# A hybrid trunk's state-space prologue: plain f32 input product, rotation tables on VectorE alone, 1/rms at the eviction, states turned back through the operators

## Chip, cores and metric

The kernel runs on one core of a Trainium2 chip. The metric is the device time of one execution in microseconds; the time before is the median of three runs. Engines are called as in the profile: PE is TensorE's matmul, PEld its weight load, DVE is VectorE, ACT is ScalarE, POOL is GpSimd, SP is SyncE, which issues most transfers.

## The reference

A decoder trunk of two layers over 1024 tokens of 1024 features, all in float32. Layer 0 mixes tokens with a diagonal state-space model (S5), layer 1 with sparse attention; a squared-ReLU MLP of width 4096 stands behind each, and each of the four parts is normalised before and after. What the change touches is the mixer of layer 0:

```python
def s5_mixer(h, w_in, ...):              # h = rms_norm(x, g)
    u = (h @ w_in).reshape(bsz, seq, 32 groups, 16 channels)
    abar = exp((lr + i li) dt)           # per group and state (64 states)
    bbar = (abar - 1) / (lr + i li) * b
    bu = einsum(u, bbar)
    xs = associative_scan(x_t = abar x_(t-1) + bu_t)
    y = einsum(xs.re, c.re) - einsum(xs.im, c.im) + d_skip * u
    z = gelu(y)
    z = z * sigmoid(z @ w_glu)
    return z @ w_out
```

The norm is `x * rsqrt(mean(x^2) + eps) * g`.

## The kernel before, in words

The program is written with a tile framework that orders each engine's instructions ahead of time and puts in the semaphores; on the chip each engine works its list in order and waits where a semaphore says so. A transfer is issued by an engine's queue, in order too.

The sequence is taken in 128 chunks of 8 steps. The S5 part (`s5`, L669 and on) does this:

- **Input product** (`s5_in`): for four pairs of steps `sp`, x times w_in, eight tiles of 128 features deep, 512 columns wide. Products of the kernel are made from two float32r parts per operand, (hi, lo), with three instructions each (`mm3`, L138 to L143: hi hi, hi lo, lo hi). ACT makes hi of x (L134) and of w_in with the norm's gain (L574); DVE or POOL make lo (L135, L575). The norm's 1/rms comes from squares of a token-major copy (L592, ACT) and a short chain on DVE and ACT (`rsqrt`, L149 to L153). For `sp` 0 to 2 it is put in later, in six DVE steps (L596); for `sp` 3 at the eviction from PSUM (L604).
- **Parameters** (`s5_params`): exponentials, cosines and powers of [128, 32] tiles, several hundred small DVE instructions (L331 to L491).
- **Rotations** (`s5_rotations`): tables of cosines and sines over the chunks, in seven doubling steps of three instructions (L509 to L511), each step on 16 m numbers per partition for m = 1, 2, 4, .., 64. Half 0 (for operators 0 and 2) is made on DVE, half 1 (for 1 and 3) on POOL. ACT spreads them (L513 to L515).
- **Operators** (`s5_operators`, four times, `o0` to `o3`): L525 to L527 on DVE, then 8 products of 16 columns (L535) and 8 transposes (L536) on PE; T by small transfers (L547) into a tile that POOL fills with zeros (L545); G on DVE (L550 to L552).
- **States** (`s5_states`, `s0` to `s3`): U transposed (L619), products with the operator (L627 to L629), turned into a rotating frame (L630 to L632), scanned along the chunks (L636), and turned back: two ACT copies swap the halves (L639, L640), POOL multiplies by the sines (L641), DVE by the cosines (L642) and subtracts (L643).
- **Outputs** (`s5_gelu`, `g0` to `g3`): per group a product with T (L654) and one with G (L655) into one bank, gelu (L657), transposes (L663).

Products with an f32 operand that is not split (L535, L627 to L629, L654, L655) are plain f32. The gate (`g` tiles) and the output product (`p` tiles on L141 to L143 from 190 us) end the mixer; norms follow, and from 260 us on MLP and attention.

Of the kernel before, what the change touches and what calls it, by code (L numbers as in the profile page):

```python
# [35 lines left out]
def bc_mid(t, shape):  # L36
    """[p, a, c] read as [p, a, n, c]."""
    return t.rearrange("p (a o) c -> p a o c", o=1).to_broadcast(shape)


def bc_last(t, shape):
    """[p, a, b] read as [p, a, b, n]."""
    return t.rearrange("p a (b o) -> p a b o", o=1).to_broadcast(shape)


class Trunk:
# [34 lines left out]
    def p1(self, shape):  # L81
        """One bank of PSUM."""
        self.n += 1
        return self.pp.tile(shape, F32, name=f"p1_{self.n}", tag="p1", bufs=7)

    def pm(self):
        """One bank of PSUM for the MLPs."""
# [3 lines left out]
    def pg(self):  # L91
        """One bank of PSUM for the gate's sums."""
# [3 lines left out]
    def small(self, shape, dt=F32, tag="s", bufs=8):  # L96
        """A few numbers of each partition, from a ring; more than a few in a tile of their own."""
# [13 lines left out]
    def unit(self, src, last=False):  # L111
        """A weight unit of 128 x 1024 as two halves of 512 columns, each split into two f32r parts."""
# [25 lines left out]
    def mm3(self, ps, w, x, start, stop):  # L138
        """ps += w.T x for operands (hi, lo)."""
# [5 lines left out]
    def rsqrt(self, ms, n, k=1.0):  # L145
        """k / sqrt of a [128, n] tile of normal positive numbers."""
# [9 lines left out]
    def pc(self):  # L156
        """One bank of PSUM for the norms."""
# [3 lines left out]
    def squares(self, blocks, add):  # L161
        """Sums of squares of the 512 tokens of four blocks [128, 2, 512], as [128, 4] in PSUM."""
# [18 lines left out]
    def pre_norm(self, h, gi, tag="b", square=True):  # L181
        """Blocks of h -> (hi, lo) blocks of h times the norm's gain, and 1/rms of the tokens, or its square, which
        goes in behind the products."""
# [19 lines left out]
    def post_norm(self, f, gi, h, e=None, reorder=False, last=None, aside=False):  # L203
        """h + norm(f) in place of the blocks f; reorder puts tokens (s, kk) into the order of time. Where f is still
        to be scaled by r, the square of a 1/rms, e is EPS / r^2 for the sum of squares: as norm(r f) is
        f / sqrt(mean(f^2) + EPS / r^2), r itself isn't needed."""
# [51 lines left out]
    def mlp(self, L, x, side=None, per=0, wait=0, finish=None):  # L258
        """side: a generator of other work, per of its steps beside each weight unit after the first ones. finish is
        called with each half of the tokens, whose last products come one half after the other."""  # L260
# [64 lines left out]
    def exp_(self, x, n):  # L325
        """exp of a [128, n] tile."""
# [73 lines left out]
    def s5_params(self, par, dsk, em, bc):  # L400
# [36 lines left out]
        # rows 0..63 hold real parts, 64..127 imaginary ones; sg flips signs between them  # L437
# [14 lines left out]
        # powers l = 0..8  # L452
# [19 lines left out]
        # unit phasor of a whole chunk, its powers 1, 2, 4, .., 64 (cos, and -sin and sin), and the chunk's decay;  # L472
        # rows 0..63 hold the phasors of groups 0..15, rows 64..127 those of the others
# [21 lines left out]
    def s5_rotations(self, A, B, k, eng):  # L495
        """Cosines and sines over the chunks for 8 groups in A and 8 in B: worked out in A with the groups of B in
        rows 64..127, then spread."""
# [19 lines left out]
    def s5_operators(self, o):  # L517
        """Operators of eight groups."""
# [9 lines left out]
        # H[(s, c), c'] of lag 7 - s, with d_skip at lag 0  # L528
# [24 lines left out]
        r["G"] = gm  # L553
        return r

    def s5_in(self, U):
        """norm(x) @ w_in by chunk, with the norm's gain in w_in and its 1/rms put in behind the product."""
        nc, a = self.nc, self.a
        xs, wu = [], []

        def load(sp):
            xs.append([self.ld([128, 4, 256], a["xs"][sp, dh]) for dh in range(2)])

        xs.append([self.ld([128, 4, 256], a["xs"][0, 0])])
        for j in range(4):
            if j == 1:
                xs[0].append(self.ld([128, 4, 256], a["xs"][0, 1]))
            self.n += 1
            raw = self.wp.tile([128, 1024], F32, name=f"wr{self.n}", tag="wr5", bufs=4)
            nc.sync.dma_start(raw, a["w_in"][j])  # L570
            kh, kl = [self.blk([128, 2, 512], F32R, tag="x") for _ in range(2)]
            for h in range(2):
                r, gn = raw[:, h * 512:(h + 1) * 512], self.gain[:, 0, 2 * j + h:2 * j + h + 1]
                nc.scalar.activation(kh[:, h], r, AF.Copy, scale=gn)  # L574
                nc.vector.scalar_tensor_tensor(kl[:, h], r, gn, kh.bitcast(F32)[:, h], op0=ALU.mult, op1=ALU.subtract)  # L575
                wu.append((kh[:, h], kl[:, h]))
        ms = self.small([128, 8], F32, "kept")
        us = U.rearrange("p g (s c) -> p s g c", c=16)

        def scaled(k, n):  # L580
            m = self.small([128, 8], F32)
            nc.vector.tensor_scalar(m[:, :n], ms[:, k:k + n], 1.0 / 1024, EPS, op0=ALU.mult, op1=ALU.add)
            return self.rsqrt(m, n)

        for sp in range(4):
            if sp:
                load(sp)
            x = [self.split(xs[sp][dh], [128, 4, 256], lo_pool=sp > 0 or dh > 0, tag="hid") for dh in range(2)]
# [4 lines left out]
            if sp == 3:  # L593
                ri = scaled(6, 2)
                for k in range(6):
                    nc.vector.tensor_scalar(us[:, k], us[:, k], r0[:, k:k + 1], None, op0=ALU.mult)  # L596
            for s_ in range(2):
                ps = self.pm()
                for kt in range(8):
                    self.mm3(ps, [t[:, kt % 4, s_ * 128:(s_ + 1) * 128] for t in x[kt // 4]], wu[kt], kt == 0, kt == 7)  # L600
                if sp < 3:
                    nc.scalar.activation(us[:, 2 * sp + s_], ps.rearrange("p (g c) -> p g c", c=16), AF.Copy)
                else:
                    nc.scalar.activation(us[:, 2 * sp + s_], ps.rearrange("p (g c) -> p g c", c=16), AF.Copy,  # L604
                                         scale=ri[:, s_:s_ + 1])
            if sp == 2:
                r0 = scaled(0, 6)
# [685 lines left out]
```

## Time and profile before

| | |
|---|---|
| runs | 2326.21, 2325.18, 2315.68 us; median 2325.18 |
| profiled execution, span from first to last instruction | 2320.5 us |
| profiled execution, a time of its own | none on the page; the span is 4.7 us under the median of the runs |
| PE, DVE, ACT, POOL busy | 94%, 64%, 48%, 40% |
| mean granted clock of TensorE | 0.973 |

The clock is given as a share of full speed; it has two levels, 2.4 GHz (1.0) and 1.2 GHz (0.5). Busy times overlap: PE's products are pipelined, and a product's row has its latency, so the distance between starts tells what one costs in a row of them.

### The profile page before, as it was taken

To read this page: it belongs to the slowest core of one execution; us is meant where nothing else is said; L and a number is where in the kernel's file an instruction comes from. 1 tells how busy PE (TensorE), PEld (TensorE's weight loads), DVE (VectorE), ACT (ScalarE), POOL (GpSimd) and SP (SyncE) were. 2 spreads that over 40 slices of the span, in tenths; PEclk is the share of its full clock that TensorE was granted. 3 is DMA by queue.
4 is the path that set the end of the run, shared out by engine and by line. 5 is a ranking of instruction groups with operands and counts; after the bars stand their busy time and mean duration, and the time that the engine had idled before them with its cause. 6 is when DMAs were issued, how large, how long until landed. Compare 5 with 4: busy or idle time off the path is not lost.

```text
span 2320.5 us, 31662 instructions
## 1 busy us (share of the span) xinstructions
PE 2186.8 (94%) x11392; PEld 1855.6 (80%) x11392; DVE 1481.9 (64%) x2949; ACT 1105.0 (48%) x2009; POOL 928.5 (40%) x752
## 2 busy tenths in 40 slices
PE   7688999999999999999999989899999998999997
PEld 5467778888879987888878977787889887788886
DVE  9875873233562499556595899999767738433335
ACT  5435543333354565455454666666455644333332
POOL 5422552222245533444347433444555435322223
PEclk9779999999999999999999999999999999999998
DMA  7102443333345554443455524233333245433331
GB/s 259 40 20 68 141 163 93 98 100 93 97 141 167 134 128 115 112 111 94 142 180 145 145 90 109 76 88 79 87 87 79 80 130 181 136 100 93 98 100 55
DMA packets 92988, 258.47 MB, mean 111 GB/s; under 512 B 10912, under 2 KB 23584, under 8 KB 92832
## 3 DMA queue, kind: packets, MB, share of 16 engines
q1 hardware_dynamic: 79072, 232.34, 31.4%
q0 software_dynamic: 12672, 23.07, 5.5%
q8 instruction: 90, 1.47, 0.3%
q10 hardware_dynamic: 1088, 1.05, 0.1%
q14 instruction: 66, 0.54, 0.1%
HBM read 222.73 MB, written 32.51 MB: 110 GB/s over the span
## 4 chain that ended last, share of the span: by engine, by line
PE 68%; DVE 18%; ACT 5%; issue 5%; POOL 1%; DMA 1%; SPq 0%; DVEq 0%; ACTq 0%; POOLq 0%
PE m L141 17%; PE m L142 17%; PE m L143 17%; PE p L141 2%; PE p L143 2%; PE p L142 2%; PE p L1021 2%; PE p L1042 2%; DVE wh L124 2%; DVE b L234 1%; ACT junk L962 1%; PE p L891 1%; DVE b L191 1%; DVE junk L924 1%; DVE acc L234 1%
## 5 line engine op out<-in xcount | busy, mean ns | idle before, releaser
L142 PE MATMUL m<-b,wh 128*128 128x512 f32 (+1 forms) x2208 | 859.1, 390 | 10.4 <-DVE b L191 7.8
L141 PE MATMUL m<-b,wh 128*128 128x512 f32 (+1 forms) x2208 | 860.6, 391 | 7.9 <-ACT acc L316 2.9
L143 PE MATMUL m<-b,wh 128*128 128x512 f32 (+1 forms) x2208 | 857.7, 390 | 3.4 <-DVE wh L124 3.4
L124 POOL TENSOR_TENSOR wh<-wr,wh 128x512 fp32r<-128x512 f32 x318 | 439.0, 1382 | 954.7 <-ACT wh L123 916.0
L123 ACT ACTIVATE wh<-wr 128x512 fp32r<-128x512 f32 x636 | 396.8, 628 | 493.6 <-PE m L143 407.0
L142 PEld LDWEIGHTS m<-b,wh 128*128 128x128 f32 x2208 | 418.0, 189 | 93.6 <-DVE b L191 10.8
L141 PEld LDWEIGHTS m<-b,wh 128*128 128x128 f32 x2208 | 417.7, 189 | 92.5 <-ACT acc L316 4.5
L143 PEld LDWEIGHTS m<-b,wh 128*128 128x128 f32 x2208 | 417.8, 189 | 85.9 <-DVE wh L124 3.8
L124 DVE TENSOR_TENSOR wh<-wr,wh 128x512 fp32r<-128x512 f32 x318 | 268.2, 844 | 311.7 <-ACT wh L123 280.4
L318 DVE TENSOR_TENSOR acc<-acc,m 128x512 f32<-128x512 f32 x216 | 147.1, 682 | 145.5 <-PE m L143 144.0
L1029 POOL TENSOR_TENSOR s<-s,ring 128x128 f32<-128x128 f32 (+7 forms) x128 | 157.7, 1244 | 161.5 <-DVE ring L1028 140.3
L283 ACT ACTIVATE b<-m 128x512 f32<-128x512 f32 x128 | 76.2, 595 | 152.9 <-PE m L143 152.3
L132 DVE CAST b<-b 128x1024 fp32r<-128x1024 f32 x68 | 64.5, 949 | 120.4 <-ACT b L285 117.3
L141 PE MATMUL p<-wh,b 128*128 128x256 f32 x480 | 135.8, 288 | 3.0 <-ACT wh L123 3.0
L142 PE MATMUL p<-wh,b 128*128 128x256 f32 x480 | 136.4, 288 | 1.6 <-POOL wh L124 1.2
L143 PE MATMUL p<-wh,b 128*128 128x256 f32 x480 | 135.4, 286 | 0.0
L1046 ACT ACTIVATE pt<-p 128x512 fp32r<-128x512 f32 (+1 forms) x160 | 83.3, 553 | 91.0 <-PE p L1042 84.9
L1027 ACT ACTIVATE s<-s,ring 128x128 f32<-128x128 f32 (+7 forms) x128 | 98.6, 772 | 50.8 <-DVE ring L1025 46.9
L1023 DVE CUSTOM_DVE_ANT_0 s<-p,nb 128x512 f32<-128x512 f32 (+3 forms) x192 | 100.3, 550 | 34.6 <-PE p L1021 29.8
L1047 DVE TENSOR_TENSOR pt<-p,pt 128x512 fp32r<-128x512 f32 (+1 forms) x160 | 99.0, 630 | 30.5 <-ACT pt L1046 30.1
L962 ACT ACTIVATE junk<-b,ring 128x512 bf16<-128x512 f32 (+2 forms) x90 | 80.8, 898 | 73.0 <-DVE ring L958 67.2
L1021 PE MATMUL p<-kt,q 128*128 128x256 f32 x640 | 104.9, 293 | 5.0 <-DVE acc L318 2.4
(306 smaller groups left out, 3229.2 us busy)
## 6 DMA issues: line engine op xcount, KB each, us to landing
wr<-in_w_dram SPq DMA_DIRECT2D x256, 512.0 KB, 3.6
wr<-in_wa_dram SPq DMA_DIRECT2D x32, 512.0 KB, 3.7
q<-qd POOLq DMA_DIRECT2D x64, 256.0 KB, 5.4
ld<-hd SPq DMA_DIRECT2D x24, 512.0 KB, 6.7
hd<-b SPq DMA_DIRECT2D x16, 512.0 KB, 4.5
qd<-qt SPq DMA_DIRECT2D x32, 256.0 KB, 3.4
wr<-in_wao_dram SPq DMA_DIRECT2D x16, 512.0 KB, 3.6
q<-qi POOLq DMA_DIRECT2D x24, 256.0 KB, 4.7
```

What stands on the lines that cost most here:

```text
L123: nc.scalar.activation(hi, r, AF.Copy)
L124: (nc.gpsimd if h else nc.vector).tensor_sub(lo, r, hi.bitcast(F32))
L141: mm(ps, w[0], x[0], start=start, stop=False)
L142: mm(ps, w[0], x[1], start=False, stop=False)
L143: return mm(ps, w[1], x[0], start=False, stop=stop)
L318: nc.vector.tensor_add(acc[d][:, j], acc[d][:, j], ps)
L962: nc.scalar.activation(junk[:, 1, :W[j]], keys[j].bitcast(F32), AF.Sign, bias=neg[:, j:j + 1], accum_out=cnt[:, j:j + 1])
L1021: nc.tensor.matmul(ps[:, 256 * e:256 * e + 256], qt[:, v, 2 * hp + k, :], self.K[2 * c + e][:, g, :], start=v == 0, stop=v == 1)
L1023: nc.vector.tensor_tensor_reduce(out=s[:, a:a + n], in0=ps[:, :n], in1=nb[:, a:a + n], scale=1.0, scalar=-BIG, op0=ALU.add, op1=ALU.max, a ...
L1027: nc.scalar.activation(s, s, AF.Exp, bias=ng[:, k, 0:1], scale=0.125, accum_out=sm[:, k, 0:1])
L1029: nc.gpsimd.tensor_tensor(s, s, rc[:, k, 0:1].to_broadcast([128, W]), op=ALU.mult)
L1047: nc.vector.tensor_sub(pl[:, :nk], pt[:, :nk], ph.bitcast(F32)[:, :nk])
```

## The change

Six things change, all in the S5 part; comments and docstrings are gone as well, so that lines from L596 of the old file on stand eight lower in the new one.

- The input product takes x and w_in (with the gain) as plain f32: one instruction where there were three, without splits of x and w_in. w_in gets the gain in place (ACT). x is loaded into the buffers that the splits had.
- 1/rms is worked out for each pair of steps and put in at each eviction from PSUM; the six DVE steps are gone.
- Both halves of the rotation tables are made on DVE.
- The sums of the turned states (old L632) are DVE's for all four sets.
- States are no longer turned back after the scan. DVE multiplies the scanned states by sines into one tile and by cosines in place; the swap of halves and the difference are left to PE, which adds a third product per group, with an operator `Gs` that is G with its halves swapped (two ACT copies per set of operators).
- `s5_states` returns that second tile too.

```diff
@@ s5_operators @@
-        r["G"] = gm
+        nc.scalar.activation(t[0:64], gm[64:128], AF.Copy)
+        nc.scalar.activation(t[64:128], gm[0:64], AF.Copy)
+        r["G"], r["Gs"] = gm, t
@@ s5_in @@
...
-            raw = self.wp.tile([128, 1024], F32, name=f"wr{self.n}", tag="wr5", bufs=4)
-            nc.sync.dma_start(raw, a["w_in"][j])
-            kh, kl = [self.blk([128, 2, 512], F32R, tag="x") for _ in range(2)]
+            w = self.blk([128, 2, 512], tag="x")
+            nc.sync.dma_start(w, a["w_in"][j].rearrange("p (h n) -> p h n", h=2))
             for h in range(2):
-                r, gn = raw[:, h * 512:(h + 1) * 512], self.gain[:, 0, 2 * j + h:2 * j + h + 1]
-                nc.scalar.activation(kh[:, h], r, AF.Copy, scale=gn)
-                nc.vector.scalar_tensor_tensor(kl[:, h], r, gn, kh.bitcast(F32)[:, h], op0=ALU.mult, op1=ALU.subtract)
-                wu.append((kh[:, h], kl[:, h]))
+                gn = self.gain[:, 0, 2 * j + h:2 * j + h + 1]
+                nc.scalar.activation(w[:, h], w[:, h], AF.Copy, scale=gn)
+                wu.append(w[:, h])
...
         for sp in range(4):
+            squares(sp)
             if sp:
                 load(sp)
-            x = [self.split(xs[sp][dh], [128, 4, 256], lo_pool=sp > 0 or dh > 0, tag="hid") for dh in range(2)]
...
-            if sp == 3:
-                ri = scaled(6, 2)
-                for k in range(6):
-                    nc.vector.tensor_scalar(us[:, k], us[:, k], r0[:, k:k + 1], None, op0=ALU.mult)
+            m = self.small([128, 8], F32)
+            nc.vector.tensor_scalar(m[:, :2], ms[:, 2 * sp:2 * sp + 2], 1.0 / 1024, EPS, op0=ALU.mult, op1=ALU.add)
+            r = self.rsqrt(m, 2)
             for s_ in range(2):
                 ps = self.pm()
                 for kt in range(8):
-                    self.mm3(ps, [t[:, kt % 4, s_ * 128:(s_ + 1) * 128] for t in x[kt // 4]], wu[kt], kt == 0, kt == 7)
...
+                    nc.tensor.matmul(ps, xs[sp][kt // 4][:, kt % 4, s_ * 128:(s_ + 1) * 128], wu[kt],
+                                     start=kt == 0, stop=kt == 7)
+                nc.scalar.activation(us[:, 2 * sp + s_], ps.rearrange("p (g c) -> p g c", c=16), AF.Copy,
+                                     scale=r[:, s_:s_ + 1])
@@ s5_states @@
-            (nc.gpsimd if o else nc.vector).tensor_add(z[:, s], z[:, s], t[:, s])
+            nc.vector.tensor_add(z[:, s], z[:, s], t[:, s])
...
-        Z, Zs, C, S = X[:, :, 1:128], t[:, :, 1:128], C[:, :, 0:127], S[:, :, 0:127]
-        nc.scalar.activation(Zs[0:64], Z[64:128], AF.Copy)
-        nc.scalar.activation(Zs[64:128], Z[0:64], AF.Copy)
-        nc.gpsimd.tensor_mul(Zs, Zs, S)
-        nc.vector.tensor_mul(Z, Z, C)
-        nc.vector.tensor_sub(Z, Z, Zs)
-        return ut, X
+        nc.vector.memset(t[:, :, 0:1], 0.0)
+        nc.vector.tensor_mul(t[:, :, 1:128], X[:, :, 1:128], S[:, :, 0:127])
+        nc.vector.tensor_mul(X[:, :, 1:128], X[:, :, 1:128], C[:, :, 0:127])
+        return ut, X, t
@@ s5_gelu @@
                 nc.tensor.matmul(py[:, i, :], X[:, g, :], r["G"][:, g].rearrange("p t c -> p (t c)"),
+                                 start=False, stop=False)
+                nc.tensor.matmul(py[:, i, :], Xs[:, g, :], r["Gs"][:, g].rearrange("p t c -> p (t c)"),
                                  start=False, stop=True)
@@ s5 @@
-        self.s5_rotations(*CS, 1, nc.gpsimd)
+        self.s5_rotations(*CS, 1, nc.vector)
```

The framework orders each engine's list anew, and in the mixer the lists differ beyond the lines edited. Behind the mixer they are the same but for a few neighbours on PE in one place.

On PE, the end of the input product (`m` tiles), the second operator (L535 and L536 into `p_85`, `p_87`) and the first transposes of U (L619), before:

```order
L143 MATMUL m_668<-b_115,b_621 128x512
L535 MATMUL p_85_699<-b_426,b_694 128x16
L536 MATMUL p_87_701<-con,b_694 128x128
L536 MATMUL p_88_711<-con,b_694 128x128
L619 MATMUL p_93_739<-con,U_84 128x128 x4
L627 MATMUL p_97_753<-b_738,b_512 128x128
```

The same place now; the second operator is `p_69`, `p_71`, `p_72`, and the input product L595 (each row x2 is two of a bank's eight instructions):

```order
L595 MATMUL m_196<-b_101,ld_188 128x512 x2
L535 MATMUL p_46_387<-b_302,b_382 128x16
L535 MATMUL p_69_531<-b_302,b_526 128x16
L536 MATMUL p_72_543<-con,b_526 128x128
L595 MATMUL m_206<-b_87,ld_186 128x512 x2
L595 MATMUL m_506<-b_87,ld_496 128x512 x2
L595 MATMUL m_516<-b_87,ld_496 128x512 x2
L595 MATMUL m_516<-b_101,ld_498 128x512 x2
L611 MATMUL p_77_573<-con,U_84 128x128 x4
```

The second operator stood behind the whole product; now three banks, 24 of its 64 instructions, stand behind the second operator.

On DVE, the last doubling step of the rotations and what follows it up to the second operator's L527, now (`b_428` is the table; before, one L509, L510 and L511 of each size stood here and the others on POOL):

```order
L509 TENSOR_TENSOR b_428<-b_428,tb_216 128x2x8x64
L510 TENSOR_TENSOR b_430<-b_428,tb_216 128x1024
L510 TENSOR_TENSOR b_460<-b_428,tb_216 128x1024
L511 TENSOR_TENSOR b_428<-b_428,b_430 128x2x8x64
L511 TENSOR_TENSOR b_428<-b_428,b_460 128x2x8x64
L550 TENSOR_TENSOR b_421<-tb_216,b_302 128x1024
L525 TENSOR_TENSOR b_526<-tb_216,b_301 128x1024
L527 TENSOR_TENSOR b_526<-b_526,b_527 128x1024
```

Both halves alternate on DVE in each step.

On DVE, between the scans of the first states (`b_787` before, `b_621` now) and those of the second, before and then now:

```order
L636 SCALAR_TENSOR_TENSOR b_787<-tb_340,b_751 128x127 x4
L630 TENSOR_TENSOR b_815<-p_107_817,b_550 128x512
L642 TENSOR_TENSOR b_787<-b_787,b_550 128x8x127
L636 SCALAR_TENSOR_TENSOR b_851<-tb_340,b_815 128x127 x4
L643 TENSOR_TENSOR b_787<-b_787,b_752 128x8x127
```

```order
L628 SCALAR_TENSOR_TENSOR b_621<-tb_216,b_585 128x127 x4
L622 TENSOR_TENSOR b_647<-p_91_649,b_428 128x512
L632 TENSOR_TENSOR b_586<-b_621,b_428 128x8x127
L624 TENSOR_TENSOR b_647<-b_647,b_648 128x512
L633 TENSOR_TENSOR b_621<-b_621,b_428 128x8x127
L628 SCALAR_TENSOR_TENSOR b_683<-tb_216,b_647 128x127 x4
```

What PE's outputs wait for was L643, between the second set's scans; it is now L633, ahead of all of them.

## Rows read from the trace of the kernel before

**Rows 1.** The page: busy us, mean ns of one, idle before.

```profile
L283 ACT ACTIVATE b<-m 128x512 f32<-128x512 f32 x128 | 76.2, 595 | 152.9 <-PE m L143 152.3
```

**Rows 2.** Busy time by stretch: engines, PEclk, DMA share, GB/s.

```profile
4.60:82.30 77.70, 55.88 (x216) 43.43 (x216) 76.58 (x204) 42.48 (x63) 52.00 (x32) 0.88 0.57 209
...
145.70:166.00 20.30, 19.78 (x85) 13.90 (x84) 15.33 (x17) 2.81 (x5) 6.78 (x4) 0.50 0.15 42
...
260.00:2320.50 2060.50, 1982.33 (x10410) 1694.77 (x10408) 1283.86 (x2579) 985.52 (x1828) 819.42 (x680) 0.99 0.38 112
```

**Rows 3.** Groups of DVE from 4.6 to 82.3 us, columns as rows 1.

```profile
L482 DVE TENSOR_TENSOR sb<-tb 128x16 f32<-128x16 f32 x9 | 7.7, 855 | 0.0
L511 DVE TENSOR_TENSOR b<-b,b 128x16 f32<-128x16 f32 (+6 forms) x7 | 7.4, 1054 | 0.0
L575 DVE SCALAR_TENSOR_TENSOR b<-wr,con,b 128x512 fp32r<-128x512 f32 x8 | 6.0, 748 | 0.8 <-ACT b L574 0.8
...
L509 DVE TENSOR_TENSOR b<-b,tb 128x16 f32<-128x16 f32 (+6 forms) x7 | 3.9, 557 | 0.0
...
L483 DVE TENSOR_TENSOR sb<-tb 128x16 f32<-128x16 f32 x9 | 1.5, 162 | 0.0
```

**Rows 4.** Groups of POOL in the same stretch.

```profile
L135 POOL TENSOR_TENSOR b<-ld,b 128x1024 fp32r<-128x1024 f32 x7 | 19.3, 2753 | 21.4 <-ACT b L134 21.4
L511 POOL TENSOR_TENSOR b<-b,b 128x16 f32<-128x16 f32 (+6 forms) x7 | 10.5, 1500 | 0.3
...
L545 POOL MEMSET b<- 128x1024 f32 x1 | 1.0, 956 | 0.0
```

**Rows 5.** PE in order of time, 82 to 123 us: start, duration, [idle before].

```profile
82.40 0.58 PE L535 MATMUL p<-b,b 128*128 128x16 f32 x2 [8.96 <-DVE b L527]
...
86.55 0.45 PE L536 MATMUL p<-con,b 128*128 128x128 f32 x1
...
91.23 1.97 PE L619 MATMUL p<-con,U 128*128 128x128 f32 x8 [4.23 <-ACT U L604]
...
101.31 0.49 PE L627 MATMUL p<-b,b 128*128 128x128 f32 x2 [0.25 <-ACT b L620]
...
107.61 0.71 PE L654 MATMUL p<-b,b 128*128 128x128 f32 x4
114.32 0.79 PE L655 MATMUL p<-b,b 128*128 128x128 f32 x2 [6.00 <-DVE b L643]
...
122.42 1.93 PE L535 MATMUL p<-b,b 128*128 128x16 f32 x16 [0.98 <-ACT b L664]
```

**Rows 6.** DVE in order of time, 96 to 114 us.

```profile
96.56 0.69 DVE L630 TENSOR_TENSOR b<-p,b 128x512 f32<-128x512 f32 x1 [6.83 <-PE p L627]
...
102.57 1.36 DVE L636 TENSOR_TENSOR_SCAN b<-tb,b 128x127 f32<-128x127 f32 x4
...
113.08 1.19 DVE L643 TENSOR_TENSOR b<-b,b 128x1016 f32<-128x1016 f32 x1
```

**Rows 7.** PE in order of time, 137 to 190 us.

```profile
137.55 0.39 PE L654 MATMUL p<-b,b 128*128 128x128 f32 x2
137.78 0.39 PE L655 MATMUL p<-b,b 128*128 128x128 f32 x2
...
144.67 0.37 PE L535 MATMUL p<-b,b 128*128 128x16 f32 x2 [2.49 <-DVE b L527]
...
152.43 0.74 PE L627 MATMUL p<-b,b 128*128 128x128 f32 x2
...
163.20 0.80 PE L142 MATMUL g<-b,wh 128*128 128x512 f32 x1
...
176.60 0.80 PE L655 MATMUL p<-b,b 128*128 128x128 f32 x2 [1.02 <-DVE b L643]
...
190.00 1.66 PE L141 MATMUL p<-b,wh 128*128 128x512 f32 x6 [0.82 <-ACT b L713]
```

**Rows 8.** POOL in order of time, 170 to 171 us.

```profile
170.47 3.32 POOL L641 TENSOR_TENSOR b<-b,b 128x1016 f32<-128x1016 f32 x1 [5.06 <-issue]
```

More of the change, by code (lines that the diff above doesn't have):

```diff
@@ L558, in s5_in, with squares @@
         nc, a = self.nc, self.a
-        xs, wu = [], []
+        xs, wu, sq = [], [], []
         def load(sp):
[L562 to L568, printed above, removed]
-            raw = self.wp.tile([128, 1024], F32, name=f"wr{self.n}", tag="wr5", bufs=4)
-            nc.sync.dma_start(raw, a["w_in"][j])
-            kh, kl = [self.blk([128, 2, 512], F32R, tag="x") for _ in range(2)]
-            for h in range(2):
-                r, gn = raw[:, h * 512:(h + 1) * 512], self.gain[:, 0, 2 * j + h:2 * j + h + 1]
-                nc.scalar.activation(kh[:, h], r, AF.Copy, scale=gn)
-                nc.vector.scalar_tensor_tensor(kl[:, h], r, gn, kh.bitcast(F32)[:, h], op0=ALU.mult, op1=ALU.subtract)
-                wu.append((kh[:, h], kl[:, h]))
[L577 to L587, printed above, removed]
-            x = [self.split(xs[sp][dh], [128, 4, 256], lo_pool=sp > 0 or dh > 0, tag="hid") for dh in range(2)]
+            xs.append([self.ld([128, 4, 256], a["xs"][sp, dh], "hid") for dh in range(2)])
+        def squares(sp):
             for s_ in range(2 * sp, 2 * sp + 2):
@@ L592, in s5_in @@
                 nc.scalar.activation(q, q, AF.Square, accum_out=ms[:, s_:s_ + 1])
-            if sp == 3:
-                ri = scaled(6, 2)
-                for k in range(6):
-                    nc.vector.tensor_scalar(us[:, k], us[:, k], r0[:, k:k + 1], None, op0=ALU.mult)
+        xs.append([self.ld([128, 4, 256], a["xs"][0, 0], "hid")])
+        for j in range(4):
+            if j == 1:
+                xs[0].append(self.ld([128, 4, 256], a["xs"][0, 1], "hid"))
+            w = self.blk([128, 2, 512], tag="x")
+            nc.sync.dma_start(w, a["w_in"][j].rearrange("p (h n) -> p h n", h=2))
+            for h in range(2):
+                gn = self.gain[:, 0, 2 * j + h:2 * j + h + 1]
+                nc.scalar.activation(w[:, h], w[:, h], AF.Copy, scale=gn)
+                wu.append(w[:, h])
+        ms = self.small([128, 8], F32, "kept")
+        us = U.rearrange("p g (s c) -> p s g c", c=16)
+        for sp in range(4):
+            squares(sp)
+            if sp:
+                load(sp)
+            m = self.small([128, 8], F32)
+            nc.vector.tensor_scalar(m[:, :2], ms[:, 2 * sp:2 * sp + 2], 1.0 / 1024, EPS, op0=ALU.mult, op1=ALU.add)
+            r = self.rsqrt(m, 2)
             for s_ in range(2):
@@ L599, in s5_in @@
                 for kt in range(8):
-                    self.mm3(ps, [t[:, kt % 4, s_ * 128:(s_ + 1) * 128] for t in x[kt // 4]], wu[kt], kt == 0, kt == 7)
[L601 to L607, printed above, removed]
+                    nc.tensor.matmul(ps, xs[sp][kt // 4][:, kt % 4, s_ * 128:(s_ + 1) * 128], wu[kt],
+                                     start=kt == 0, stop=kt == 7)
+                nc.scalar.activation(us[:, 2 * sp + s_], ps.rearrange("p (g c) -> p g c", c=16), AF.Copy,
+                                     scale=r[:, s_:s_ + 1])
             yield
@@ L637, in s5_states, with s5_gelu @@
                                          z[:, g, 0:127], 0.0, op0=ALU.mult, op1=ALU.add)
-        Z, Zs, C, S = X[:, :, 1:128], t[:, :, 1:128], C[:, :, 0:127], S[:, :, 0:127]
-        nc.scalar.activation(Zs[0:64], Z[64:128], AF.Copy)
-        nc.scalar.activation(Zs[64:128], Z[0:64], AF.Copy)
-        nc.gpsimd.tensor_mul(Zs, Zs, S)
-        nc.vector.tensor_mul(Z, Z, C)
-        nc.vector.tensor_sub(Z, Z, Zs)
-        return ut, X
-    def s5_gelu(self, o, r, ut, X):
+        nc.vector.memset(t[:, :, 0:1], 0.0)
+        nc.vector.tensor_mul(t[:, :, 1:128], X[:, :, 1:128], S[:, :, 0:127])
+        nc.vector.tensor_mul(X[:, :, 1:128], X[:, :, 1:128], C[:, :, 0:127])
+        return ut, X, t
+    def s5_gelu(self, o, r, ut, X, Xs):
         nc = self.nc
```

## The prediction

> **What bounds the kernel now.** I read the busy time by stage first [rows 2]. From 260 us to the end TensorE (PE) is busy 1982 of 2060 us: a product behind a product. None of that is edited, and on VectorE (DVE), ScalarE (ACT), GpSimd (POOL) and SyncE the order behind the mixer is the same in both kernels (on PE but for a few neighbours in one place), so what the prologue gives or takes moves the end one for one. The question is when the mixer's output products start: 190.0 us now [rows 7].
>
> Then DVE in the first stretch: from 4.6 to 82.3 us it is busy 76.6 of 77.7 us [rows 2]; its groups [rows 3] show why. L482 and L483 are the same 128x16 shape, yet one averages 855 ns and the other 162; the L511 steps of the rotations take 7.4 us for what L509 does in 3.9. Beside them POOL splits x and builds the second rotation table [rows 4]: a DVE instruction that meets one of POOL's waits until it is over. Summed over the thirteen groups that show it, the excess over the same shape undisturbed is 29.5 us (L482 alone 9 x 0.69 = 6.2). PE waits for the end of this work: L535 at 82.40 after 9.0 us idle, for L527, the second operator.
>
> Last, PE's own order of time from there [rows 5, 7]: first transposes of U at 91.23; first output products with turned states at 114.32 after 6.0 us of waiting for L643; second operators 144.67; last states 152.43 to 163.20, at half clock; last outputs 176.60 after another wait for L643; 190.00 the end of the stage.
>
> **The change part by part.** Times are of the profiled execution.
>
> *DVE up to the second operator.* 77.6 us now (4.64 to 82.25). Gone: the 29.5 us of excess, L575 (8 spaced 0.67 us, and 0.8 us of waiting [rows 3]: 6.2), and one split of x, 1.1. Added: the second rotation table. L509 is 3.9 us for seven steps, one of them lengthened by 0.75; less 0.08 us of overlap each, a clean set is 2.6, three sets 7.8 (at most 3 x 3.9 = 11.7). POOL keeps three weight splits that still hold DVE up, about 1.2 us each: 3.6. Two more small 1/rms chains: 1. Sum 77.6 - 29.5 - 6.2 - 1.1 + 7.8 + 3.6 + 1 = 53.2, so L527 ends near 57.8 instead of 82.3. Were none of the excess to go it would be 87.3; half, 72.5.
>
> POOL keeps its fills of the operators (L545, 0.96 us each [rows 4]) too. I count none of the two that fall in this stretch; if they held DVE up as POOL's products do, the sum would be 1.9 us later, 2310. The Trainium skill (SBUF — State Buffer, section "Who interferes with whom") says that DVE and GpSimd lock a pair of ports for a whole instruction, and that an instruction of DVE with two inputs in memory meets one of GpSimd that reads there, not one that only writes. By that rule the fills cost nothing and the excess goes as a whole, which speaks against the rival below that leaves half of it.
>
> *The plain product.* A plain f32 product of 128 columns takes 0.2225 us at full clock (137.55 to 137.78 holds one, as two instructions [rows 7]). 512 columns were not seen: 4 x 0.2225 = 0.89 if all of it scales, 0.85 if a fixed part of some 10 ns does not; I take 0.86. Sixty-four of them are 55 us. The order rows decide what that means: forty stand ahead of the first operator, and take 8 to 45 us under DVE's work; but the second operator now stands ahead of the last 24. Those cannot start before 57.8 + 4.4 (L535 and L536 after a long wait, 82.40 to 86.55 and one more [rows 5]) = 62.2, and last 20.6: 82.8. One eviction, 0.6 as L283's [rows 1], and the first transposes start at 83.4: 7.8 us earlier than 91.23, not the 24 by which DVE is earlier. ACT has some 25 us of copies and squares after DVE's tables (48 us or so), hence ends first, near 76.
>
> *States to outputs, first pair.* Now 114.32 - 91.23 = 23.1. Transposes 1.3, two sets of states 6.3 each at full clock (101.31 to 107.61 [rows 5]). Then DVE alone decides: per half set two products out of PSUM and a sum of 0.6 us spacing, four scans 1.36 together, and the two multiplications of 1.13 that now end the turning [rows 6]. ACT's two copies, POOL's product and DVE's subtraction behind them are gone. Placed in DVE's new order (first half at +4.7, second at +7.8, the second set's evictions between), the second multiplication ends at +18.0. Gain 5.1. The sums that POOL made (L632) are DVE's in this, 0.6 us each.
>
> *Outputs.* Each of four sets gets eight more plain products of 0.2225: 1.8 us. In the first set the cover is nil: -1.8. From its end to the second operators' start (122.42 to 144.67 now, 22.3) I get 25.4: the second set's 1.8, and 1.3 because DVE's cast for the gate stands behind more of its own work. -3.1.
>
> *Last states.* Now 152.43 to 163.20, 10.8 us, in a stretch granted 0.50 [rows 2]; the same work at full clock was 6.3. After a wait of 2.3 us I let PE be slow for the gate's four products and the operators (6 us, as after the other waits), then full: +0.3 and +4.5.
>
> *From the last states to the last outputs.* Now 163.20 to 176.60, 13.4: scans, two ACT copies, POOL's 3.32 [rows 8], then L643. In its place: the second half's evictions and scans 4.3, two multiplications 2.3, with the third set's outputs (24 x 0.2225 = 5.4) and transposes beside them: 8.3. Gain 5.0. To 190.0 another 13.4 now; 14.4 then (1.8 for the last set, less 0.8 since PE comes without a wait). -1.0.
>
> *At nothing:* eight copies of ACT for the swapped operators (1.05 each) stand where four pairs of state copies stood, and ACT has over half its time free; the scaling at eviction replaces L596's six DVE steps after the operators. Transfers are the same bytes in nearly the same queue order, and x goes to buffers that the splits had.
>
> **Sum.** 7.8 + 5.1 - 1.8 - 3.1 + 0.3 + 4.5 + 5.0 - 1.0 = 16.8 us: output products at 173.2, span 2320.5 - 16.8 = 2303.7 [rows 2]. The median of the runs is 4.7 above the span; 2325.2 - 16.8 = 2308.
>
> **Rivals.** *The clock stays low until the last states are done* (2315). For: the row at 0.50, the same order of small work ahead. It costs the 4.5, 1.0 on eight transposes and 1.6 on eight gate products: gain 9.7. For it too: PE was busy 19.8 of 20.3 us in that stretch and the clock didn't rise. Against: the gate's second twelve products all stand before these states now, where eight of them stood behind.
>
> *DVE isn't freed* (2323): half of the excess is its own, and the tables end at 72.5. The transposes start 14.7 later than I say, at 98.1: gain 2.1. For: short steps like L482 are lengthened too, not only large ones. Against: the same shape beside them at 162 ns.
>
> *Plain products at half clock* (2352, slower). Place: the 64 of the prologue; price 0.85 us for each at half. If all of them: forty end at 77, both operators 8.8, 24 x 1.71 = 41, an eviction 0.6: transposes at 127.5 instead of 83.4, so 44 lost against 17 won: 27 slower. It eats the gain from the twentieth of the last 24 on (20 x 0.85 = 17); those alone at half clock end at 2329, no change, and the first forty have 12 us of DVE's work over them. For: the clock fell after every wait in rows 5, and 9 us of waiting remain ahead of the 24. Against: output products of the same kind reached 0.2225 us within one set [rows 7].
>
> *Better than I say* (2303): no slow stretch after waits, operators 2.3 instead of 4.4 twice and the gate's 0.8.
>
> **How the numbers follow.** Forecast 0.48, low clock 0.25, DVE not freed 0.12, half-clock products 0.05, better 0.10. About 0.5%, 11.6 us, is what a measurement of this kernel can tell from no change; that bound is 2313.6. Forecast, 6 us either way, gives faster 0.46, same 0.02; the low clock 0.08 and 0.17; DVE not freed 0.01, 0.09 and slower 0.02; half clock same 0.01, slower 0.04; better 0.10. In sum faster 0.65, same 0.29, slower 0.06. The range takes in the low clock and DVE half freed on one side and the better case with the runs' spread of 10.5 us on the other: 2293 to 2324; the likeliest alone is 2302 to 2314.
>
> **What would show it.** Right: DVE's L482 near 0.16 us throughout; L527 of the second operator ending at 55 to 60; 24 plain products of about 0.86 us back to back from 62, U's transposes at 83; first outputs 18 us after; output products at 173; all later rows shifted by the same amount. Wrong: tables that end after 70; a plain product spaced over 1 us beyond the first few; last states of 10 us; a shift at 260 us that is not found again at the end.

## The result, and the profile after

The changed kernel takes 2305.43 us (median of six runs, 2301.02 to 2311.69); the kernel before 2317.97 us, in six runs too. The ratio is 0.9938, with a 95% interval of 0.9917 to 0.9960: faster by 0.6%, or 12.5 us. Run once more beside other runs of before, it gave 2305.39 against 2319.31 us and 0.9935 (0.9914 to 0.9956). The forecast was 2308 us.

Three executions of the changed kernel were traced, and they differ in one place. The first, the slowest of its six runs (2311.69 us), lost 5 us there; the other two (2303.8 us, the fastest of its six runs, and 2303.15 us) agree within 0.6 us at the operators, the transposes, the first outputs and the output products. I read the second trace first.

Lines of the new kernel: L597 is the old L604 (eviction into U), L611 the old L619 (transposes of U), L619 the old L627 (states), L632 and L633 are DVE's two multiplications (old L642 is now L633), L644 and L645 the old L654 and L655 (outputs), and L647 is the third product.

Its groups of DVE up to the second operator, 4.6 to 57 us (line, operation, count, busy us and mean ns, idle before):

```profile
L484 DVE TENSOR_TENSOR tb<-sb 128x16 f32<-128x16 f32 x9 | 3.7, 411 | 0.0
L482 DVE TENSOR_TENSOR sb<-tb 128x16 f32<-128x16 f32 x9 | 2.6, 290 | 2.1 <-ACT tb L477 2.1
...
L511 DVE TENSOR_TENSOR b<-b,b 128x16 f32<-128x16 f32 (+6 forms) x14 | 5.9, 455 | 0.0
L483 DVE TENSOR_TENSOR sb<-tb 128x16 f32<-128x16 f32 x9 | 1.5, 168 | 0.1
```

L482, 855 ns on average in [rows 3], is at 290, and L511 takes 5.9 us for fourteen steps where seven took 7.4. What is left of the excess is three instructions, each beside one of POOL's weight splits; the others of L482 and L484 take 0.16 or 0.17 us:

```profile
23.44 1.27 DVE L484 TENSOR_TENSOR tb<-sb 128x16 f32<-128x16 f32 x1
...
28.66 1.26 DVE L484 TENSOR_TENSOR tb<-sb 128x16 f32<-128x16 f32 x1
...
31.93 1.26 DVE L482 TENSOR_TENSOR sb<-tb 128x16 f32<-128x16 f32 x1
```

Each is lengthened by 1.1 us, 3.3 together (3.6 forecast). POOL's fills (L545, at 33.10 and 48.64) lengthen none, which is what the Trainium skill (SBUF — State Buffer, section "Who interferes with whom") has of a GpSimd instruction that only writes.

PE in order of time in the second trace (start, duration, [idle before, and what ended it]), the rows that answer to [rows 5, 7]; a plain product is two instructions, so x48 is the 24:

```profile
56.95 0.61 PE L535 MATMUL p<-b,b 128*128 128x16 f32 x2 [8.37 <-DVE b L527]
...
61.38 22.90 PE L595 MATMUL m<-b,ld 128*128 128x512 f32 x48
...
85.06 1.10 PE L611 MATMUL p<-con,U 128*128 128x128 f32 x8 [0.78 <-ACT U L597]
...
102.61 0.49 PE L645 MATMUL p<-b,b 128*128 128x128 f32 x2 [1.49 <-DVE b L633]
...
111.98 0.37 PE L535 MATMUL p<-b,b 128*128 128x16 f32 x2 [0.78 <-ACT b L656]
...
134.94 0.44 PE L535 MATMUL p<-b,b 128*128 128x16 f32 x2
...
144.26 0.38 PE L619 MATMUL p<-b,b 128*128 128x128 f32 x2
...
150.46 0.49 PE L644 MATMUL p<-b,b 128*128 128x128 f32 x2
...
158.15 0.39 PE L645 MATMUL p<-b,b 128*128 128x128 f32 x2
...
172.53 1.66 PE L141 MATMUL p<-b,wh 128*128 128x512 f32 x6 [0.83 <-ACT b L705]
```

Each is a stage of the prediction: second operator, the 24 plain products, U's transposes, first outputs with turned states, third operator, fourth, last states and their end, last outputs, output products. 190.00 in [rows 7] has become 172.53, 17.5 us earlier. Behind it, in these two traces, nothing is lost. ACT's L283, which follows the MLP's products, in before and then in the second trace:

```profile
L283 ACT ACTIVATE b<-m x128: 573/598/622, 260.9 to 2258.3; 128x512 f32<-128x512 f32 x128
```

```profile
L283 ACT ACTIVATE b<-m x128: 571/598/622, 243.4 to 2239.8; 128x512 f32<-128x512 f32 x128
```

The first of the 128 is 17.5 us earlier, the last 18.5, the spans 18.5 (2320.5, 2302.0). The medians differ by only 12.5 to 14. The rest lies in which executions were traced: before's runs take 1.7 to 1.9 us more than their spans, so its traced execution took some 2322.3 us (an estimate: 2320.5 and 1.8), 3 to 4 above its medians of 2317.97 (six runs) and 2319.31 (23 others), and the second trace is 1.6 under the median of its own runs.

Now the first trace, at the place where it differs:

```profile
55.29 0.61 PE L535 MATMUL p<-b,b 128*128 128x16 f32 x2 [7.84 <-DVE b L527]
...
64.65 0.47 PE L536 MATMUL p<-con,b 128*128 128x128 f32 x1 [6.61 <-ACT b L537]
...
66.52 22.77 PE L595 MATMUL m<-b,ld 128*128 128x512 f32 x48
90.06 1.09 PE L611 MATMUL p<-con,U 128*128 128x128 f32 x8 [0.78 <-ACT U L597]
...
177.55 1.66 PE L141 MATMUL p<-b,wh 128*128 128x512 f32 x6 [0.81 <-ACT b L705]
```

In the middle of the second operator PE waits 6.6 us for ACT to empty a bank (L537). What held ACT, in its own order of time:

```profile
62.88 1.06 ACT L571 ACTIVATE b<-b 128x1024 f32<-128x1024 f32 x1 [11.34 <-DMA b<-in_xt_dram]
63.84 0.19 ACT L571 ACTIVATION_READ_ACCUMULATOR b<-b 128x1 f32 x1
63.93 0.19 ACT L150 ACTIVATE ring<-ring 128x2 f32<-128x2 f32 x1
64.02 0.57 ACT L537 ACTIVATE b<-p 128x512 f32<-128x512 f32 x1
```

A square of the token-major copy of x stands ahead of L537 and waits 11.3 us for its load. The load is late because of what stands ahead of it on SP's queue, the loads of w_so, which wait for a buffer that POOL's split L124 still reads. What SP's queue waited for (total us, times, longest), its order, and POOL's:

```profile
SPq L116 <- POOL wh L124: 26.9, 3, 23.3
```

```profile
27.57 0.43 SPq L1152 DMA_DIRECT2D con<-in_rope_dram  x1
51.98 4.73 SPq L116 DMA_DIRECT2D wr<-in_w_so_dram  x3
56.81 0.86 SPq L570 DMA_DIRECT2D b<-in_xt_dram  x2
```

```profile
23.22 33.15 POOL L124 TENSOR_TENSOR wh<-wr,wh 128x512 fp32r<-128x512 f32 x3 [22.76 <-ACT wh L123]
```

Three splits take 33.15 us, the first 28.7. In the second trace the first takes 1.43:

```profile
23.25 1.43 POOL L124 TENSOR_TENSOR wh<-wr,wh 128x512 fp32r<-128x512 f32 x1 [22.80 <-ACT wh L123]
27.53 5.63 POOL L124 TENSOR_TENSOR wh<-wr,wh 128x512 fp32r<-128x512 f32 x2 [2.85 <-ACT wh L123]
```

Same program, same start; once POOL was shut out while DVE ran 71 instructions without a pause (27.68 of 27.68 us busy), once it got in at the next one. That DVE's stream is what held POOL is read from these rows; in the second trace DVE runs without a pause there as well (5.80 of 5.80 us from 23.2), so the stream alone does not decide it. When the experiments began, only the trace with the long split was at hand.

### The profile page after: what moved, and what is told of

It reads as the page before. It is cut to its first block, busy times and chain, and to the rows that moved or that the text cites. A ratio compares the mean times of both kernels' runs of the same rounds, so it can differ in the third digit from the quotient of the medians.

```text
span 2309.9 us, 31616 instructions
## 1 busy us (share of the span) xinstructions
PE 2194.5 (95%) x11392; PEld 1844.8 (80%) x11392; DVE 1451.1 (63%) x2977; ACT 1097.7 (48%) x2003; POOL 889.4 (39%) x712
## 4 chain that ended last, share of the span: by engine, by line
PE 72%; DVE 15%; issue 5%; ACT 5%; POOL 1%; DMA 0%; SPq 0%; DVEq 0%; ACTq 0%; POOLq 0%
PE m L141 17%; PE m L143 17%; PE m L142 17%; PE p L1013 2%; PE p L141 2%; PE p L143 2%; PE p L142 2%; PE p L1034 2%; DVE wh L124 1%; DVE b L234 1%; PE p L1043 1%; DVE b L191 1%; PE p L1042 1%; PE p L883 1%; DVE acc L234 1%
## 5 line engine op out<-in xcount | busy, mean ns | idle before, releaser
L124 POOL TENSOR_TENSOR wh<-wr,wh 128x512 fp32r<-128x512 f32 x318 | 467.1, 1470 | 1004.9 <-ACT wh L123 962.3
L124 DVE TENSOR_TENSOR wh<-wr,wh 128x512 fp32r<-128x512 f32 x318 | 269.3, 848 | 307.3 <-ACT wh L123 284.4
L283 ACT ACTIVATE b<-m 128x512 f32<-128x512 f32 x128 | 76.3, 596 | 154.6 <-PE m L143 153.9
L132 DVE CAST b<-b 128x1024 fp32r<-128x1024 f32 x68 | 60.9, 896 | 122.0 <-ACT b L285 117.7
L1038 ACT ACTIVATE pt<-p 128x512 fp32r<-128x512 f32 (+1 forms) x160 | 83.5, 554 | 92.1 <-PE p L1034 90.1
```

Of the source, the lines that this page charges most:

```text
L124: (nc.gpsimd if h else nc.vector).tensor_sub(lo, r, hi.bitcast(F32))
L1038: nc.scalar.activation(ph[:, :nk], pt[:, :nk], AF.Copy)
```

## The experiments

Each kernel is the changed one with the edit shown, unless it says "before". Outputs start at the time in its trace at which PE begins the output products; ratios are against the kernel before, with 95% intervals.

| kernel | transposes of U | outputs start | median us | ratio |
|---|---|---|---|---|
| before | 91.2 | 190.0 | 2318 to 2320 | 1 |
| changed (three traces) | 90.1, 85.1, 84.6 | 177.6, 172.5, 172.0 | 2305.4 | 0.9938 (0.9917 to 0.9960) |
| splits on DVE | 82.1 | 172.5 | 2306.7 | 0.9949 (0.9934 to 0.9964) |
| copies on ACT's queue | 78.0 | 164.4 | 2295.6 | 0.9905 (0.9888 to 0.9923) |
| old turning | 86.0 | 182.4 | 2320.6 | 1.0004 (0.9989 to 1.0019) |
| before, plain product alone | 89.8 | 188.7 | 2325.0 | 1.0026 (1.0016 to 1.0037) |
| rotations on POOL | 90.9 | 176.8 | 2311.7 | 0.9965 (0.9951 to 0.9979) |
| before, turning alone | 93.0 | 189.1 | 2323.7 | 1.0010 (0.9996 to 1.0025) |
| ACT's queue and banks | 81.7 | 172.0 | 2303.4 | 0.9923 (0.9901 to 0.9944) |
| copies first | 72.4 | 164.5 | 2296.4 | 0.9883 (0.9862 to 0.9905) |
| copies first, banks | 71.0 | 161.4 | 2294.8 | 0.9882 (0.9863 to 0.9902) |
| step by way of PSUM (one run) | 78.5 | 164.3 | 2295.0 | none |

Runs of one kernel lie up to 11 us apart, those of before up to 20, and the intervals are some 2 to 5 us to either side, so medians closer than that don't rank kernels. Traces show where time went, but each is one execution.

**Is it POOL's split that holds SP's queue?** First three weight units split on DVE alone (`wn` counts them):

```diff
-            (nc.gpsimd if h else nc.vector).tensor_sub(lo, r, hi.bitcast(F32))
+            (nc.gpsimd if h and self.wn >= 3 else nc.vector).tensor_sub(lo, r, hi.bitcast(F32))
```

> The changed kernel, with the six half-splits (L124) of the first three weight units all on DVE, three of them off POOL. Theory (POOL's first split, 28.7 us long beside DVE's unbroken stream, holds a weight buffer, SP's queue stands behind it with the token-major copies of x, ACT stands behind the squares with L537, and PE behind L537): SP issues the three w_so loads near 31 us instead of 52, the last copies of x are in by 50, PE does not wait for L537 any more; second operator's L527 near 57 (three splits of 0.6 more), 4.4 for its products, 20.5 for the 24 plain products, U's transposes at 82 to 83 instead of 90.1, output products 7 us earlier than 177.6, time about 2299. Rival (the copies are late for transfer congestion or for their own two buffers): L537 still waits past 60 us, transposes at 89 to 92, time 2305 or a little above.

It went as the theory has it up to the transposes: SP issued the w_so loads from 28.45 us, PE didn't wait for L537, and the transposes came at 82.12. By itself this does not show the chain, since unedited executions go the same way (below); the waits of the first trace above do. Outputs start 5 us earlier than in the first trace, not 7: PE waits 2.4 us for DVE ahead of the third operator and is at half clock behind it. But the median is no better than the changed kernel's, 2306.7 against 2305.4. That raised the question whether the first trace was typical, and the unedited kernel ran again:

> The changed kernel once more, unedited. The kernel with the splits on DVE put its output products 5 us earlier in the trace than the changed kernel's trace, and yet its median is no better. Theory (POOL's long split is there in every execution, and the two medians differ by the scatter between chips and sessions): again a first split of over 20 us on POOL, PE waits 6 to 7 us for L537, transposes at 89 to 91, output products at 177 to 178; median beside the same runs of before 12 to 13 us lower. Rival (POOL is let in earlier in other executions, and the profiled one was an unlucky one): transposes at 82 to 84 in this trace, output products near 171.

The rival held: POOL was let in at once, and outputs start at 172.53. So the waiting chain costs 5.0 us between these two traces (177.55 less 172.53). How often it comes is not known; that the median without it (splits on DVE) is no better speaks for seldom. A third trace:

> The changed kernel a third time, one look. One trace had POOL's first split at 28.7 us, one at 1.4, and the kernel with the old turning, whose DVE order is the same there, at 24.0. If being shut out is a matter of phase between the two engines, any of 1.3 to 29 us can come, and the rest follows: over 20 us gives transposes at 88 to 91 and output products at 177 to 178, under 5 us gives 84 to 86 and 172 to 173.

First split 1.36 us, transposes 84.55, outputs 172.01: the second kind again.

**The copies on another queue**, with the split left where it is:

```diff
-                nc.sync.dma_start(q, a["xt"][s_])
+                nc.scalar.dma_start(q, a["xt"][s_])
```

> The changed kernel, with the token-major copies of x loaded by ACT's queue instead of SP's; POOL's split stays where it is. The framework then sets all 64 plain products ahead of the second operator. Theory (SP's queue is what held the copies): squares end before 50 us although POOL's split still takes over 20 us; products end near 65 to 68, second operator right behind, U's transposes at 68 to 72 instead of 90.1, output products near 158, time about 2286. Rival (what holds the copies is POOL's split itself or the transfers): squares still past 60 us, transposes at 85 or later, time 2300 or more.

POOL's three splits took 5.7 us together this time, so it says nothing on the chain. The gain comes from the order: with all products ahead of the second operator PE has no wait of 8 us any more. Transposes are at 77.99, not at 68 to 72, and outputs at 164.4, not 158: the first copies are now loaded and squared ahead of w_in, ACT puts the gain into w_in from 14.85 us after 6.2 us of waiting for a load, and the first product starts at 15.62 instead of 8.7. The median is 10 us under the changed kernel's.

**The parts by themselves.** States turned back the old way (the product's and the tables' edits stay):

```diff
-        nc.vector.tensor_mul(t[:, :, 1:128], X[:, :, 1:128], S[:, :, 0:127])
-        nc.vector.tensor_mul(X[:, :, 1:128], X[:, :, 1:128], C[:, :, 0:127])
-        return ut, X, t
+        nc.scalar.activation(Zs[0:64], Z[64:128], AF.Copy)
+        nc.scalar.activation(Zs[64:128], Z[0:64], AF.Copy)
+        nc.gpsimd.tensor_mul(Zs, Zs, S)
+        nc.vector.tensor_mul(Z, Z, C)
+        nc.vector.tensor_sub(Z, Z, Zs)
+        return ut, X
```

> The changed kernel, with states turned back as before (two ACT copies, POOL's product, DVE's subtraction, two products per group, state sums of the last three sets on POOL). By the stages of the changed kernel's trace the turning back through the operators is worth 5.5 us at the first outputs and 5.7 at the last, and costs 1.3, 0.8 and 1.0 between: without it output products 8 us later (about 186), time about 2313. Rival (the gain of those stages came from DVE being free, not from the turning): output products at 178 to 180, time 2305 to 2308.

```profile
107.97 0.80 PE L645 MATMUL p<-b,b 128*128 128x128 f32 x2 [5.94 <-DVE b L633]
```

The wait for the subtraction is back with its old length (6.00 in [rows 5]); outputs start 9.9 us later than in the changed kernel's usual trace, 4.9 later than in its first. POOL's first split took 24.0 us here, and still PE waited only 0.7 us for L537. Both forecasts missed: outputs lie between the two, and the median is 15 us above the changed kernel's, more than the 9.9. Measured against before it brings nothing, though its trace starts the outputs 7.6 us earlier. Of these, 7.3 are left at the first of ACT's L283 (253.6 for 260.9), 4.0 at the last (2254.3 for 2258.3), and the traced execution of before was itself 3 to 4 us late. Why 3.3 us go behind the mixer stays open.

The kernel before with the new `s5_in` alone:

> The kernel before, with the plain f32 input product and 1/rms at the eviction alone; second rotation table on POOL, states turned back the old way. Theory: the tables still meet POOL's, so the second operator's L527 ends at 60 to 68 instead of 82.3, and the 24 products behind it (20.5 us) with the waits eat that: transposes at 87 to 93, output products at 186 to 192, time 2313 to 2319, hence no change. Rival (the plain product alone brings the gain): transposes at 80 to 84, time 2305 to 2309.

Right in the trace: L527 of the second operator is waited for until 62.52, and the 24 products (66.94 to 89.0) eat that. In time it is a little worse than before, 1.0026, and 6 us above the expected range; the trace, of one of its faster executions, doesn't show why.

The kernel before with `Gs`, two DVE multiplications and three products per group alone:

> The kernel before, with the turning back through the operators alone (swapped operators, two DVE multiplications, three products per group, all state sums on DVE). Theory (this part gives the whole gain of the change): U's transposes at 91 as before, first outputs 5 to 6 us sooner behind them, the last outputs 5 to 6 sooner behind the last states, 2 to 3 lost between: output products at 180 to 183 instead of 190, time 8 to 10 us under the kernel before. Rival (it needs the freed DVE): gain of 0 to 3 us.

The rival was nearer. The wait of 6.0 us ahead of the first outputs is gone, and they come at 114.5, no earlier than before: U's transposes come 1.8 us later, behind a wait of 6.4 us for the last scaling, and the first states run at half clock. In time nothing is gained (1.0010). Busy time by stretch there, and for the same work in before (engines, granted clock, DMA share, GB/s):

```profile
93.00:107.40 14.40, 14.39 (x64) 9.54 (x64) 5.61 (x12) 1.79 (x3) 0.00 (x0) 0.50 0.00 1
```

```profile
91.20:101.30 10.10, 9.82 (x64) 6.75 (x64) 4.02 (x9) 1.83 (x4) 0.00 (x0) 0.83 0.04 10
```

The second table back on POOL:

```diff
-        self.s5_rotations(*CS, 1, nc.vector)
+        self.s5_rotations(*CS, 1, nc.gpsimd)
```

> The changed kernel with the second rotation table back on POOL. Theory (DVE's tables end later, near 62 instead of 55, as in the kernel before with the plain product alone, but POOL's splits end by 38, so the copies of x are early and PE does not wait for L537): second operator 62 to 67, 24 products, transposes at 88 to 90 as now, output products within 2 us of 177.6, time within 3 us of the changed kernel, so that the table on DVE is worth nothing in this kernel as it stands. Rival (the table on DVE is worth its 7 us of DVE): transposes at 96 to 98, time 2312.

Against the first trace the theory's outputs hold (176.8 and 177.6), but not its time; against the usual one the table on DVE is worth 5.7 us at the second operator (62.67 instead of 56.95), 5.8 at the transposes and 4.3 at the outputs, and 2311.7 instead of 2305.4 in time.

**No waits at all up to the transposes.** ACT's queue for the last three pairs of copies, and the last four banks of the product from those of the gate:

```diff
-                nc.sync.dma_start(q, a["xt"][s_])
+                (nc.scalar if sp else nc.sync).dma_start(q, a["xt"][s_])
-                ps = self.pm()
+                ps = self.pm() if sp < 2 else self.pg()
```

> The changed kernel, with the copies of x of the last three pairs loaded by ACT's queue and the input product's last four banks taken from the gate's banks, so that no product waits for an eviction. All 64 products then stand ahead of the second operator's. Theory (PE itself is the bound up to the transposes once no wait is left: first product at 8.7, 64 spaced 0.92, two sets of operators 2.3 each at full clock): transposes at 71 to 74, output products near 158 (86.4 us behind, as in the kernel with the copies on ACT's queue), time about 2289. Rival (DVE or ACT becomes late: rotation tables and 1/rms): transposes at 78 or later, time 2295 or more.

```profile
69.61 9.59 PE L595 MATMUL g<-b,ld 128*128 128x512 f32 x16 [6.68 <-DVE b L543]
```

A miss, with transposes at 81.67 and a time of 2303.4. The banks were those of the first operator: a product waits until DVE's L543 has read one, and DVE stands behind a square root on ACT. Then the squares first, with four buffers:

```diff
-"sq5": 2
+"sq5": 4
+        for sp in range(4):
+            squares(sp)
         for sp in range(4):
-            squares(sp)
```

> The changed kernel, with the squares of all four pairs of steps ahead of the products in the program and four buffers for them instead of two: the copies of x then stand ahead of the last weight loads on SP's queue, the squares ahead of the table's copies on ACT, and 56 of 64 plain products ahead of the second operator. Theory (up to U's transposes PE's own work is the bound once it waits for nothing: first product at 8.7, 64 spaced 0.92, two sets of operators of 2.3): transposes at 72 to 75 instead of 85, output products 87 to 90 later (159 to 165), time 2288 to 2296, below the kernel with the copies on ACT's queue. Rival (another wait comes in its place, for the second operator's L527 or a bank): transposes at 80 or later, time 2300 or more.

The copies now stand ahead of the w_so loads on SP, and the squares ahead of the table's copies on ACT. Transposes at 72.41 and outputs at 164.5, as expected; the time of 2296.4 is just above its range. With the gate's banks besides:

> As the kernel with the squares first, and the input product's last four banks taken from the gate's, so that all 64 products stand ahead of the second operator. Theory (PE-bound): transposes at 72 to 75, as without the banks, time 2288 to 2296. Rival (as in the kernel with ACT's queue and banks, a product waits some 7 us for a bank that the first operator still holds): transposes at 79 to 82, time 2300 to 2304.

```profile
54.09 13.90 PE L596 MATMUL g<-b,ld 128*128 128x512 f32 x32
...
71.03 1.09 PE L612 MATMUL p<-con,U 128*128 128x128 f32 x8 [0.75 <-ACT U L598]
...
161.35 1.67 PE L141 MATMUL p<-b,wh 128*128 128x512 f32 x6 [0.68 <-ACT b L706]
```

PE waits nowhere from the first product, at 8.21, up to the 0.75 us ahead of the transposes, and the clock is 1.00 all the way. Outputs start 11 us earlier than in the changed kernel, and the median, 2294.8, is 10.6 lower: 1.2% under before, level with the others near 2296. Its trace, of the slowest of its six runs, ends only 5.0 us earlier (span 2297.0 for 2302.0). Part of what is lost goes at the MLP's start, in PE's waits from 160 to 320 us:

```profile
PE m L143 <- POOL wh L124: 5.7, 1, 5.7
```

In the kernel without the banks the longest wait there is 3.7 us; PE now arrives ahead of the weights.

**What lets POOL in.** A step of the tables by way of PSUM (`t` is the product that L511 adds):

```diff
             o, t = A[:, :, g, m:2 * m], tmp[:, :, :, :m]
+            if k and j == 3:
+                t = self.p1([128, 2, 8, 8])
```

> The changed kernel, with one doubling step of the second rotation table (m = 8, near 33 us on DVE) made by way of a bank of PSUM: one product writes it, one sum reads it. In the trace with the long split POOL was let in right behind the first DVE instruction that reads PSUM (L543, 50.76 us). Theory (such an instruction lets POOL in): if POOL's first split begins before 30 us and isn't let in at once, it ends within 2 us of that step, near 35, and SP's weight loads follow. Rival (it is something else about 50 us): shut out until 46 to 52 us again. Should POOL get in at once, the look tells nothing on this.

POOL got in at once (1.48 us), so it decides nothing. The edit moved the order as well: the second table is ended behind the second operator's work on DVE, and on PE 16 products instead of 24 stand behind that operator. In this one run outputs came at 164.3.

## Why the prediction was right, step by step

Gains in the second trace, each the stage's length now against the length in [rows 5, 7]:

| step | forecast | measured |
|---|---|---|
| second operator's L535 (its time) | 57.8 | 56.95 |
| U's transposes | +7.8 | +6.2 (91.23, 85.06) |
| to the first outputs | +5.1 | +5.5 (23.1, 17.55) |
| first outputs to third operator | -1.8 | -1.3 (8.1, 9.37) |
| to the fourth operator ("the second operators' start") | -3.1 | -0.7 (22.25, 22.96) |
| to the last states | +0.3 | -1.6 (7.76, 9.32) |
| last states | +4.5 | +4.6 (10.77, 6.20) |
| to the last outputs | +5.0 | +5.7 (13.4, 7.69) |
| to the output products | -1.0 | -1.0 (13.4, 14.38) |
| sum | +16.8 | +17.5 |

*DVE up to the second operator* was right: L527 ended at 56.9 (57.8 forecast), with 3.3 us of splits (3.6). *The plain product* was mis-sized at its end. The price held: sixteen in a row take 13.90 us with one latency in it (the row at 54.09 above), so 0.86 each. But PE came out of its wait at half clock, and the 24 took 22.9 instead of 20.6. Stretches of the second trace:

```profile
61.40:84.40 23.00, 22.88 (x49) 9.66 (x48) 4.29 (x14) 14.27 (x23) 0.00 (x0) 0.91 0.13 36
136.00:149.00 13.00, 13.00 (x72) 10.43 (x72) 5.30 (x8) 5.02 (x7) 1.26 (x1) 0.69 0.24 74
```

0.91 over 23 us is 4.1 us at half clock, worth 2.1. The second row is the same error ahead of the last states: I let PE be slow for 6 us after its wait, and it was for some 10 (0.50 from 134 to 144 us, 8 of them in this row), hence -1.6 for +0.3. The states themselves ran at full clock, as the forecast said against its first rival.

*To the fourth operator*: I had put 1.3 us on DVE's cast for the gate and 1.8 on the products, and 0.7 was lost. PE now waits 1.86 us there, for DVE's L132 (the gate's cast), where it waited 2.49 for L527 in [rows 7]; products that stand ahead of such a wait shorten it. I take this for the reason, and no run of its own shows it.

*At nothing* was the step that can fail. "Transfers are the same bytes in nearly the same queue order" is true, and so is that POOL keeps three splits; what I left out is that the last copies of x stand behind loads that wait for such a split, and an operator's bank behind those copies on ACT. In the first trace, where DVE shuts POOL out, that costs 5 us. I had considered that POOL holds DVE up, and not that DVE can hold POOL up.

Luck had a part in how near the numbers came. The sum misses by 0.7 us because its largest misses, +2.4, -1.6 and -1.9, largely cancel. In the first trace the gain was 12.5 (190.00 less 177.55). And 2308 stands on the median of before's first three runs, 2325.18, and on a gain of 16.8; before's median of six runs is 2317.97, from which 16.8 gives 2301.2, and the medians differ by 12.5. A start 7.2 us too high and a gain 4.3 too large left a miss of 3.

The rivals: the low clock until the last states are done didn't come; DVE was freed; the plain products were not at half clock but for the first few.

The parts do not add up: plain product alone 1.3 us in the trace, turning alone 0.9, the two together 13.2 (rotations on POOL), all three 17.5. Each part alone hands its gain to the next wait (the 24 products behind L527), or to a low clock behind it (the first states at 0.50). In medians neither part alone gains anything.

## What to carry to other kernels

- A shared engine's relief is worth what the next wait leaves: place each gain at the instruction that waits, and look what stands ahead of that instruction on its own queue, loads of other things included.
- A short row on an engine that competes for a resource (POOL's 1.4 us here) has a long tail: look whether a queue stands behind it, and move what is urgent ahead of it. The copies placed ahead of the weight loads, and products ahead of an operator that waits, were worth 10 us more, with no arithmetic changed.
- One trace is one execution. Where a kernel's traced run is its slowest, trace it again before explaining a loss.

## What the runs showed of the hardware

- A POOL instruction of 1.4 us took 28.7 us in one execution and 24.0 in that of another kernel with the same DVE order, while DVE ran without a pause (71 instructions in 27.68 us; 65 in 22.8 of the 24.0), and 1.4, 1.4 and 1.5 us in three executions of the same order up to there. The Trainium skill (SBUF — State Buffer, section "Who interferes with whom") has the one engine block the other for a whole instruction; these two rows show it going on over many. In the kernel before DVE is as busy (72.34 of 72.51 us) and no POOL instruction takes over 3.7 us; what decides isn't settled.
- The plain f32 product costs PE more than three float32r instructions: 0.86 us for 512 columns against 0.69 (three starts 0.23 apart, in the gate's products), both at full clock. What it saves is on DVE, POOL and ACT.
- A wait of 6 to 8 us on PE is paid twice: in every such place of these traces the clock is at 0.50 behind it, for 4 to 14 us. Shorter waits were followed by it too: 0.50 from 134 to 144 us behind the 1.86 us at 133.45 in the second trace (PE was busy 3.5 of the 6 us before 134), and from 146 to 165 behind the 2.49 us at 144.67 in before.
